# The 56 expert tiles whose first layer is computed early: spread over the dense loop instead of standing at its head

## The chip, the cores and the metric

The kernel runs on one core of a Trainium2 chip. A core has a matrix engine (TensorE, PE in the profile), a vector engine (VectorE, DVE), an engine for activation functions (ScalarE, ACT), a general engine (GpSimd, POOL), a queue engine that only issues transfers (SyncE, SP), and 16 DMA engines that all queues share. The metric is the time of one execution on the device, in microseconds (us); the lower, the better. Each engine works through its own list of instructions in a fixed order, and semaphores hold an instruction back until what it needs is there.

## The reference, cut to what matters

One layer of a hybrid model for two streams of tokens: P (256 prompt tokens) and Q (1024 sample tokens). A token mixer comes first, which this change leaves alone. Then comes PEER, a mixture of 16384 one-neuron experts: each token picks 8 x 16 = 128 experts, and

```python
u = u_tab[idx]
act = jax.nn.gelu(jnp.einsum("td,thkd->thk", xb, u).astype(jnp.float32))
v = v_tab[idx]
return jnp.einsum("thk,thkd->td", (g * act).astype(xb.dtype), v)
```

`u_tab` and `v_tab` hold 16384 rows of 1024 floats each, 64 MiB a table. The result is added to the residual and layer-normed.

## The kernel before, in words

PEER is done in two ways at once.

**Dense.** The first five blocks of 128 tokens of stream Q (`DB = 5`, 640 tokens) go through all experts as matrix products. The 16384 experts are cut into 128 tiles of 128. For tile `n` the first layer (`first_layer`) multiplies a 128 x 1024 tile of `u_tab` (`raw<-in_peer_uT`, split into a high and a low half `uh`, `ul`) with the tokens `hTh`, `hTl`: 2 column halves of 320 tokens, 8 slices of the model dimension, 3 products of halves, so 48 matmuls with 320 columns. A Gelu on ScalarE gives `a`. `weighted(n)` multiplies `a` with the routing weights of the tile, `gt`, which lie in DRAM (`GD`), and splits the product into `wh`, `wl`. `second_layer` multiplies four tiles at a time with the matching tiles of `v_tab` (`vh`, `vl`): 5 token blocks x 2 halves of the output x 4 tiles x 3 products, so 120 matmuls with 512 columns. VectorE adds each result to the accumulators (`acc`, L1108).

The loop over `c` in `dense` makes 32 passes of four tiles. Within pass `c` the four `weighted` calls stand first each time, and the second layer of pass `c - 1` is put between them: token blocks 0 to 2 behind the first, blocks 3 and 4 behind the second. The `v` tiles of pass `c` are loaded and split from the second on; they have four buffers, all of them in use until the second layer of pass `c - 1` ends. The untreated `raw` tiles of `v` have two buffers.

**Early tiles.** For 56 of the 128 tiles (`PRE * 4`, with `PRE = 14`) the first layer is computed ahead of the loop, while the routing and the spreading of the weights of stream Q keep the other engines busy (L1246, L1247); their `a` goes to DRAM (`AD`). In the loop `weighted(n)` only loads it back (L1115). Which tiles these are is what the change touches.

**Gathered.** Stream P's two blocks and Q's blocks 5 to 7 (`experts`) fetch each token's own rows: per block 128 gathers of 128 rows of 4 KB from `in_peer_u` (L1010, issued by GpSimd) with a product and sum on VectorE each (L1023, `row<-row,h`), a Gelu, then 128 gathers from `in_peer_v`, each added with its weight on VectorE (L1032, `y<-row,act,y`). The landing buffers (`row`) are five. After a block's last `y`, `finish` does the layer norm (L984 to L997). Beside the dense loop run the last rows of `in_peer_v` for block 5 and all of blocks 6 and 7, some 580 gathers.

The kernel is written as straight code; a scheduler, which works with an estimate of its own for each duration, lays out every engine's list before the run. So the order in which dense and gathered instructions follow each other on VectorE and GpSimd is fixed when the program is built. `elt` deals the low-half splits (`ul`, `wl`, `vl`, L193) out to VectorE and GpSimd in turn, by a running count of its calls.

After the loop, `dense` multiplies the accumulators with a gate, adds the residual (L1129 on GpSimd, L1130 on VectorE), adds the last pass's products (L1105, L1106), and norms them (L992 to L996).

Of the kernel before, what the change touches and what calls it, by code (L numbers as in the profile page):

```python
# [20 lines left out]
P = 128  # L21
# [3 lines left out]
NK = 128  # L25
# [8 lines left out]


DB = 5
PRE = 14
ADA = 4
MPACE = [(i, ("w_in", int(44 + i * 0.6))) for i in range(16)]
TP, TB = 1, 3  # L40
# [59 lines left out]
def body(ctx, tc, A, O):  # L100
    nc = tc.nc
# [11 lines left out]
    SQ = Stream("Q", 1024, 1, False, "left")  # L113
# [8 lines left out]
    def numbers(pool, n, w):  # L122

        t = pool.tile([P, n, w], BF, name=f"numbers{n}")
        nc.vector.tensor_copy(t[:], iota_k[:, 0:n, None].to_broadcast([P, n, w]))
        return t
# [10 lines left out]
    def bank(s, banks=None):  # L137
        n = count["bank"] = count["bank"] + 1
        banks = banks or s.banks
        return banks[n % len(banks)].tile([P, 512], F32, tag="bank", name=f"bank{n}")  # L140

    def mm(out, terms):
        ops = []
        for l, r in terms:
            if len(l) == 1:
                ops.append((l[0], r[0]))
            else:
                ops += [(l[0], r[0]), (l[0], r[1]), (l[1], r[0])]
        for i, (l, r) in enumerate(ops):
            nc.tensor.matmul(out, l, r, start=(i == 0), stop=(i == len(ops) - 1))  # L150
# [33 lines left out]
    def elt(share):  # L184

        count["lo"] += 1
        n = count["lo"]
        return nc.gpsimd if int(n * share) != int((n - 1) * share) else nc.vector
# [6 lines left out]
    def split(pool, src, shape, tag, bufs=None, eng=None):  # L195
        hi = pool.tile(list(shape), F32R, tag=tag + "h", name=tag + "h", bufs=bufs)
        lo = pool.tile(list(shape), F32R, tag=tag + "l", name=tag + "l", bufs=bufs)
        split_into(hi[:], lo[:], src, eng or nc.gpsimd)
        return hi, lo
# [8 lines left out]
    def sub(op, *idx):  # L208
        return tuple(o[idx] for o in op)

    def dram(name, shape, dt=F32):
        return dp.tile(list(shape), dt, name="d_" + name)
# [4 lines left out]
    def tpool(s, name, bufs=1):  # L217
        return tc.tile_pool(name=name + s.name, bufs=bufs, side=s.side, reuse_waits="tile")
# [681 lines left out]
    def new_T(pool, s, nb):  # L900
        if s.native:
            return (pool.tile([P, KT, nb * P], F32, name="hT"),)
        return (pool.tile([P, KT, nb * P], F32R, name="hTh"), pool.tile([P, KT, nb * P], F32R, name="hTl"))
# [169 lines left out]
    def table(pool, src, tag, bufs, raws, eng):  # L1073

        r = pool.tile([P, D], F32, tag="raw" + tag, name="raw", bufs=raws)
        nc.sync.dma_start(r[:], src)
        return split(pool, r[:], [P, D], tag, bufs=bufs, eng=eng)

    def first_layer(s, T, n, pool, bufs, share):

        U = table(pool, A["peer_uT"][n].rearrange("p k e -> p (k e)"), "u", bufs, 2, elt(share))
        a = pool.tile([P, DB * P], F32, tag="a", name="a", bufs=2)
        for t0 in range(0, DB * P, HALF):
            ts = slice(t0, t0 + HALF)
            ps = bank(s)
            mm(ps[:, :HALF], [(sub(U, ALL, slice(k * P, (k + 1) * P)), sub(T, ALL, k, ts)) for k in range(KT)])
            nc.scalar.activation(a[:, ts], ps[:, :HALF], AF.Gelu_apprx_tanh)
        return a

    def dense(s, T, GD, AD, pool, accs, out):  # L1090
# [19 lines left out]
        def weighted(n):  # L1110
            gt = pool.tile([P, DB * P], F32, tag="gt", name="gt", bufs=3)
            nc.sync.dma_start(gt[:], GD[n])
            if n < PRE * 4:
                a = pool.tile([P, DB * P], F32, tag="a", name="a", bufs=2)
                nc.sync.dma_start(a[:], AD[n])  # L1115
            else:
                a = first_layer(s, T, n, pool, 3, 0.5)
            nc.vector.tensor_tensor(gt[:], a[:], gt[:], op=ALU.mult)  # L1118
            return split(pool, gt[:], [P, DB * P], "w", bufs=6, eng=elt(WSHARE))
# [93 lines left out]
    SQ.banks = everywhere  # L1213
    with tc.tile_pool(name="hcQ", bufs=1, side="right", reuse_waits="tile") as fp:
        hyena(SQ, Matrices(SQ, fp, MPACE), 0.4)
    GD, AD = dram("GD", [NK, P, DB * P]), dram("AD", [PRE * 4, P, DB * P])
    with tpool(SQ, "ya") as ya, tpool(SQ, "w") as wp:
        with tpool(SQ, "yb") as yb:
            halves = {0: ya, 512: yb}
# [4 lines left out]
            Td = new_T(dpool, SQ, DB)  # L1224
# [12 lines left out]
    with (tc.tile_pool(name="rq", bufs=1, side="right", reuse_waits="tile") as rq, tc.tile_pool(name="sp", bufs=1, side="right", reuse_waits="tile") as sp,  # L1237
          tc.tile_pool(name="stage", bufs=1, side="right", reuse_waits="tile") as stage, tc.tile_pool(name="dU", bufs=1, reuse_waits="tile") as up):
        SQ.banks = [pa]
        places, keys8 = numbers(rq, NCAND, TOPK), numbers(sp, NK, 8)  # L1240
        for b in ORDER:
            routes(SQ, [b], rq, places)
            if b < DB:
                spread(SQ, b, sp, stage, keys8, GD)
        SQ.banks = [pb, pc]
        for n in range(PRE * 4):  # L1246
            nc.sync.dma_start(AD[n], first_layer(SQ, Td, n, up, 2, 1)[:])  # L1247
    SQ.banks = everywhere
    ap_ = ctx.enter_context(tc.tile_pool(name="acc", bufs=1, reuse_waits="tile"))
    accs = [ap_.tile([P, D], F32, name=f"acc{b}") for b in range(DB)]  # L1250
# [171 lines left out]
```

## Time and profile before

| what | value |
|---|---|
| median of 3 runs | 5130.33 us (5128.91 to 5131.31) |
| the profiled execution, its own time | 5135.52 us |
| its span, first to last instruction | 5133.7 us |
| PE busy | 4395.7 us, 86% |
| DVE busy | 4081.8 us, 80% |
| POOL busy | 3155.0 us, 61% |
| ACT busy | 2023.5 us, 39% |

The span is what all times in the rows below count in, from its first instruction. The dense loop lies in the last 1530 us: its first matmul starts at 3616.35 us. A share of busy time is a mean over stages with different limits, so the rows below look at stretches of the loop one by one.

### The profile page before, as it was taken

What the parts mean: (1) busy time and instruction counts of PE and PEld (TensorE: products, weight loads), DVE (VectorE), ACT (ScalarE), POOL (GpSimd) and SP (SyncE); (2) the same over time, 40 slices, a digit from 0 to 9 for tenths busy, and PEclk for the clock granted to TensorE, in tenths of its full rate; (3) what the DMA queues carried; (4) which work ended last, traced back from release to release, by engine and by line L of the source; (5) the groups of instructions that cost most, each with busy time, mean ns of one, the idle gap of its engine ahead of it and who ended that gap; (6) DMA issues with size and microseconds to landing.
All of it is one profiled execution on the core that took longest, in us unless ns stands there. A gap on an engine that the chain in (4) does not pass through costs nothing.

```text
span 5133.7 us, 68153 instructions
## 1 busy us (share of the span) xinstructions
PE 4395.7 (86%) x23707; PEld 3804.8 (74%) x23707; DVE 4081.8 (80%) x6816; ACT 2023.5 (39%) x3126; POOL 3155.0 (61%) x2290
## 2 busy tenths in 40 slices
PE   6888788899999779799698887874688999999998
PEld 4676677677777678677587877773566799989997
DVE  7778564999995886566769998895688899888997
ACT  4546333336663112212434766776222222222222
POOL 1456451578886765468665576774556677667764
PEclk8999899999999889899899998995899999999999
DMA  6676646698988953478684478877988999899994
GB/s 212 218 242 196 199 144 234 214 322 293 313 305 320 312 174 99 167 290 327 231 289 153 135 238 267 290 264 245 342 314 322 333 337 340 303 343 337 337 339 155
DMA packets 608774, 1346.80 MB, mean 262 GB/s; under 512 B 63743, under 2 KB 283592, under 8 KB 607917
## 3 DMA queue, kind: packets, MB, share of 16 engines
q0 software_dynamic: 187776, 680.61, 37.7%
q1 hardware_dynamic: 412588, 648.20, 37.6%
q10 hardware_dynamic: 8064, 13.64, 0.7%
q8 instruction: 186, 3.05, 0.2%
q14 instruction: 160, 1.30, 0.1%
HBM read 1177.56 MB, written 164.68 MB: 261 GB/s over the span
## 4 chain that ended last, share of the span: by engine, by line
PE 25%; DVE 15%; DMA 6%; issue 5%; POOL 4%; ACT 3%; SPq 2%; ACTq 0%; POOLq 0%; DVEq 0%
PE bank L150 21%; PE bank L159 3%; DVE row L1023 2%; DVE hot L1058 2%; SPq L1071 2%; POOL row L1010 2%; DVE fi L951 1%; DVE y L1032 1%; DMA row<-in_peer_u,idxQ 1%; ACT G L1069 1%; DMA row<-in_peer_v,idxP 1%; POOL vl L193 1%; ACT oa L1065 1%; ACT ob L1059 1%; DVE gt L1118 1%
## 5 line engine op out<-in xcount | busy, mean ns | idle before, releaser
L1032 DVE SCALAR_TENSOR_TENSOR y<-row,act,y 128x1024 f32<-128x1024 f32 x635 | 814.5, 1283 | 146.4 <-DMA row<-in_peer_v,idxP 111.2
L1023 DVE SCALAR_TENSOR_TENSOR row<-row,h 128x1024 f32<-128x1024 f32 x640 | 762.0, 1210 | 129.2 <-DMA row<-in_peer_u,idxP 60.8
L150 PE MATMUL bank<-hTh,ul 128*128 128x320 f32 x2048 | 641.2, 315 | 16.8 <-POOL ul L193 16.7
L150 PE MATMUL bank<-hTh,uh 128*128 128x320 f32 x2048 | 643.2, 314 | 3.7 <-ACT sc L883 3.6
L150 PE MATMUL bank<-hTl,uh 128*128 128x320 f32 x2048 | 641.9, 314 | 0.0
L150 PE MATMUL bank<-vl,wh 128*128 128x512 f32 x1280 | 513.1, 401 | 50.8 <-POOL vl L193 47.4
L1010 POOL DMA_INDIRECT row<-in_peer_v,idxQ x384 | 409.8, 1067 | 230.9 <-DVE y L1032 176.3
L1010 POOL DMA_INDIRECT row<-in_peer_u,idxQ x384 | 404.9, 1054 | 230.2 <-DVE row L1023 136.3
L150 PE MATMUL bank<-vh,wh 128*128 128x512 f32 x1280 | 473.8, 397 | 76.5 <-ACT vh L192 68.5
L193 POOL TENSOR_TENSOR wl<-wr,wh 128x1024 fp32r<-128x1024 f32 x148 | 362.6, 2451 | 273.7 <-ACT wh L192 252.8
L150 PE MATMUL bank<-vh,wl 128*128 128x512 f32 x1280 | 509.3, 398 | 5.1 <-DVE wl L193 4.9
L150 PEld LDWEIGHTS bank<-hTh,ul 128*128 128x128 f32 x2048 | 390.6, 191 | 20.6 <-POOL ul L193 20.4
L150 PEld LDWEIGHTS bank<-hTh,uh 128*128 128x128 f32 x2048 | 392.0, 191 | 5.7 <-ACT sc L883 3.9
L150 PEld LDWEIGHTS bank<-hTl,uh 128*128 128x128 f32 x2048 | 392.0, 191 | 1.4
L192 ACT ACTIVATE wh<-wr 128x1024 fp32r<-128x1024 f32 x176 | 185.7, 1057 | 463.7 <-PE bank L150 187.6
L1068 PE MATMUL bank<-ob,oa 128*128 128x128 f32 x1280 | 225.6, 327 | 152.2 <-ACT G L1069 74.8
L1010 POOL DMA_INDIRECT row<-in_peer_u,idxP x256 | 272.8, 1065 | 132.3 <-DVE row L1023 73.8
L150 PEld LDWEIGHTS bank<-vh,wh 128*128 128x128 f32 x1280 | 243.8, 191 | 132.7 <-ACT vh L192 72.8
L1010 POOL DMA_INDIRECT row<-in_peer_v,idxP x256 | 277.4, 1083 | 93.7 <-issue 30.6
L150 PEld LDWEIGHTS bank<-vl,wh 128*128 128x128 f32 x1280 | 246.9, 193 | 114.1 <-POOL vl L193 56.5
L1068 PEld LDWEIGHTS bank<-ob,oa 128*128 128x128 f32 x1280 | 196.0, 226 | 179.4 <-ACT G L1069 74.7
L150 PEld LDWEIGHTS bank<-vh,wl 128*128 128x128 f32 x1280 | 246.8, 193 | 59.8 <-DVE wl L193 8.0
(442 smaller groups left out, 12457.6 us busy)
## 6 DMA issues: line engine op xcount, KB each, us to landing
raw<-in_peer_uT SPq DMA_DIRECT2D x128, 512.0 KB
raw<-in_peer_v SPq DMA_DIRECT2D x128, 512.0 KB
wr<-in_w_in SPq DMA_DIRECT2D x112, 512.0 KB
d_GD<-G SPq DMA_DIRECT2D x40, 1024.0 KB
gt<-d_GD SPq DMA_DIRECT2D x128, 320.0 KB
w<-in_w_ada SPq DMA_DIRECT2D x48, 512.0 KB
wr<-in_w_query SPq DMA_DIRECT2D x48, 512.0 KB
d_AD<-a SPq DMA_DIRECT2D x56, 320.0 KB
```

What stands on the lines that cost most here:

```text
L150: nc.tensor.matmul(out, l, r, start=(i == 0), stop=(i == len(ops) - 1))
L159: nc.tensor.matmul(out, a, b, start=(i + j == 0), stop=(i == KT - 1 and j == len(ops) - 1))
L192: nc.scalar.activation(hi, src, AF.Copy)
L193: note(eng, eng.tensor_tensor(lo, src, hi.bitcast(F32), op=ALU.subtract))
L951: nc.vector.tensor_reduce(idf[:, h, :], oh[:].rearrange("p c k -> p k c"), axis=AX.X, op=ALU.add)
L1010: i = nc.gpsimd.indirect_dma_start(out=t[:], out_offset=None, in_=A[tab], in_offset=bass.IndirectOffsetOnAxis(ap=idx[:, k:k + 1], axis=0))
L1023: nc.vector.scalar_tensor_tensor(t[:], t[:], 1.0, h[:], op0=ALU.mult, op1=ALU.mult, accum_out=act[:, k:k + 1])
L1032: nc.vector.scalar_tensor_tensor(y[:], t[:], act[:, k:k + 1], y[:], op0=ALU.mult, op1=ALU.add)
L1058: nc.vector.tensor_tensor(hot[:].rearrange("p k t q -> p k (t q)"), keys8[:], key[:, None, t0:t0 + 4, :].rearrange("p o t q -> p o (t q)") ...
L1059: nc.scalar.activation(ob[:], hot[:, :, :, 1].rearrange("p k t -> p t k"), AF.Copy)
L1068: nc.tensor.matmul(ps[:, i * P:(i + 1) * P], oa[:, i, :], ob[:, i, :], start=True, stop=True)
L1071: nc.sync.dma_start(GD[j:j + 16, :, b * P:(b + 1) * P].rearrange("j i t -> i j t"), G[:, j:j + 16, :])
```

## The change

The list `EARLY` names the tiles with an early first layer. In place of the first 56 tiles it takes the first two of every pass of four, and only the first in each fourth pass: 24 x 2 + 8 x 1 = 56. So passes 0 to 13, which computed no first layer in the loop, and passes 14 to 31, which computed four each, become passes with two, and each fourth with three. The number of early tiles, the work and the data moved stay the same.

```diff
-PRE = 14
+EARLY = [n for n in range(128) if n % 4 < (1 if n // 4 % 4 == 3 else 2)]
...
-            if n < PRE * 4:
+            if n in EARLY:
                 a = pool.tile([P, DB * P], F32, tag="a", name="a", bufs=2)
-                nc.sync.dma_start(a[:], AD[n])
+                nc.sync.dma_start(a[:], AD[EARLY.index(n)])
             else:
                 a = first_layer(s, T, n, pool, 3, 0.5)
...
-    GD, AD = dram("GD", [NK, P, DB * P]), dram("AD", [PRE * 4, P, DB * P])
+    GD, AD = dram("GD", [NK, P, DB * P]), dram("AD", [len(EARLY), P, DB * P])
...
-        for n in range(PRE * 4):
-            nc.sync.dma_start(AD[n], first_layer(SQ, Td, n, up, 2, 1)[:])
+        for i, n in enumerate(EARLY):
+            nc.sync.dma_start(AD[i], first_layer(SQ, Td, n, up, 2, 1)[:])
```

Every engine's list is the same, but for the numbers of the tiles, until the loop's first instructions; behind that the scheduler lays it out anew. Two places show how.

The first is TensorE's list in the middle of the loop, where the second layer of one pass follows that of the pass before it. `bank1203` is the last output of a pass, `bank1204` and `bank1205` are the first ones of the next; `vh_30717`, `vh_30732`, `vh_30738`, `vh_30753` are the high halves of its four `v` tiles. Before:

```order
L150 MATMUL bank1203_30701<-vl_30554,wh_30547 128x512
L150 MATMUL bank1203_30701<-vh_30553,wl_30548 128x512
L150 MATMUL bank1204_30766<-vh_30717,wh_30562 128x512
L150 MATMUL bank1205_30780<-vh_30717,wh_30562 128x512
...
L150 MATMUL bank1204_30766<-vh_30732,wh_30655 128x512
...
L150 MATMUL bank1204_30766<-vh_30738,wh_30726 128x512
...
L150 MATMUL bank1204_30766<-vh_30753,wh_30747 128x512
```

The same place in the changed kernel, where `bank1260` to `bank1263` are the outputs of two first layers, and `vh_32143`, `vh_32215`, `vh_32221`, `vh_32293` the four `v` tiles of the pass that follows:

```order
L150 MATMUL bank1260_32156<-hTh_19688,uh_32151 128x320
...
L150 MATMUL bank1263_32260<-hTh_19688,ul_32230 128x320
L150 MATMUL bank1264_32306<-vh_32143,wh_31988 128x512
L150 MATMUL bank1264_32306<-vl_32144,wh_31988 128x512
L150 MATMUL bank1264_32306<-vh_32143,wl_31989 128x512
L150 MATMUL bank1264_32306<-vh_32215,wh_32081 128x512
L150 MATMUL bank1264_32306<-vl_32216,wh_32081 128x512
L150 MATMUL bank1264_32306<-vh_32215,wl_32082 128x512
L150 MATMUL bank1264_32306<-vh_32221,wh_32209 128x512
...
L150 MATMUL bank1264_32306<-vh_32293,wh_32287 128x512
```

Between the last use of the old `v` tiles and the first use of the new ones there stood nothing; now 96 matmuls of two first layers stand there. From the pass's first second-layer matmul on, the third tile was used after 36 others and the fourth after 54; now after 6 and 33.

The second place is the end of VectorE's list, from the last accumulation of pass 30 (`bank_39691`) to the end of the program. Before:

```order
L1130 SCALAR_TENSOR_TENSOR acc_29490<-spare,acc_29490 128x1024
L1108 TENSOR_TENSOR acc_29493<-acc_29493,bank_39691 128x512
L1130 SCALAR_TENSOR_TENSOR acc_29492<-spare,acc_29492 128x1024
L193 TENSOR_TENSOR vl<-raw,vh 128x1024
...
L995 TENSOR_TENSOR acc_29493<-acc_29493,spare 128x1024
L996 TENSOR_TENSOR acc_29493<-acc_29493,spare 128x1024
L1417 UNCONDITIONAL_BRANCH
```

And in the changed kernel:

```order
L1108 TENSOR_TENSOR acc_29493<-acc_29493,bank_39691 128x512
L1032 SCALAR_TENSOR_TENSOR y<-row,act,y 128x1024
L1130 SCALAR_TENSOR_TENSOR acc_29490<-spare,acc_29490 128x1024
...
L995 TENSOR_TENSOR acc_29493<-acc_29493,spare 128x1024
L1032 SCALAR_TENSOR_TENSOR y<-row,act,y 128x1024
L996 TENSOR_TENSOR acc_29493<-acc_29493,spare 128x1024
L1032 SCALAR_TENSOR_TENSOR y<-row,act,y 128x1024 x17
L984 TENSOR_TENSOR r<-y,spare 128x1024
...
L995 TENSOR_TENSOR r<-r,spare 128x1024
L1417 UNCONDITIONAL_BRANCH
```

Before, no gathered row (`y`) is left behind that accumulation; in the changed kernel 43 are, the last 17 of them behind everything dense, and the gathered block's layer norm (L984 and what follows it) closes the program. In between, a pass with two first layers carries 17 gathered rows on VectorE and one with three carries 21, where passes 2 to 12 carried about 13 and passes 14 to 29 about 25 (fewer where one gathered block ends and the next begins).

## Rows read from the trace of the kernel before

**Rows 1.** The page, part 2: busy tenths in 40 slices of the span.

```profile
PE   6888788899999779799698887874688999999998
```

**Rows 2.** Busy time by stretch: start:end, us, each engine (instructions), PE clock, DMA share, GB/s.

```profile
3612.00:3688.00 76.00, 61.23 (x250) 48.97 (x251) 57.70 (x56) 25.47 (x33) 44.55 (x33) 0.90 0.95 353
3688.00:4064.00 376.00, 318.07 (x1283) 249.58 (x1282) 325.32 (x416) 75.86 (x90) 233.64 (x174) 0.95 0.90 326
...
4164.00:4442.00 278.00, 277.43 (x1559) 252.59 (x1558) 258.87 (x228) 69.71 (x101) 197.12 (x155) 1.00 0.94 335
...
4506.00:5006.00 500.00, 493.03 (x2763) 449.72 (x2762) 447.42 (x525) 124.77 (x181) 353.53 (x282) 0.99 0.94 339
...
5068.00:5134.00 66.00, 43.51 (x217) 37.29 (x215) 55.15 (x76) 17.13 (x24) 24.50 (x9) 0.85 0.27 103
```

**Rows 3.** Waits of PE, 3612 to 4064: us in total, times, longest.

```profile
PE bank L150 <- ACT vh L192: 68.5, 10, 52.2
PE bank L150 <- POOL vl L193: 46.8, 18, 4.9
```

**Rows 4.** Timeline of PE, single matmuls: start, us, what, idle before.

```profile
3616.35 1.22 PE L150 MATMUL bank<-vh,wh 128*128 128x512 f32 x2 [52.16 <-ACT vh L192]
...
4567.41 0.31 PE L150 MATMUL bank<-hTh,uh 128*128 128x320 f32 x1
...
4588.39 0.31 PE L150 MATMUL bank<-hTh,ul 128*128 128x320 f32 x1
...
4588.54 0.40 PE L150 MATMUL bank<-vh,wh 128*128 128x512 f32 x1
...
4604.67 0.39 PE L150 MATMUL bank<-vh,wl 128*128 128x512 f32 x1
...
5067.61 0.39 PE L150 MATMUL bank<-vh,wl 128*128 128x512 f32 x1
```

**Rows 5.** Timeline of PE, from one pass's second layer to the next, near 3760.

```profile
3756.98 0.39 PE L150 MATMUL bank<-vh,wl 128*128 128x512 f32 x1
...
3770.98 0.50 PE L150 MATMUL bank<-vl,wh 128*128 128x512 f32 x1 [2.27 <-POOL vl L193]
...
3777.53 0.50 PE L150 MATMUL bank<-vl,wh 128*128 128x512 f32 x1 [2.18 <-POOL vl L193]
```

**Rows 6.** Groups of DVE, 3612 to the end: count, busy, mean ns, idle before.

```profile
L1032 DVE SCALAR_TENSOR_TENSOR y<-row,act,y 128x1024 f32<-128x1024 f32 x324 | 415.8, 1283 | 23.3 <-DMA row<-in_peer_v,idxQ 19.2
...
L1118 DVE TENSOR_TENSOR gt<-a,gt 128x640 f32<-128x640 f32 x128 | 187.5, 1467 | 45.2 <-DMA a<-d_AD 31.1 <-ACT a L1087 9.7 <-DMA gt<-d_GD 3.2
...
L193 DVE TENSOR_TENSOR wl<-gt,wh 128x640 fp32r<-128x640 f32 x64 | 66.5, 1040 | 13.0 <-ACT wh L192 13.0
...
L1130 DVE SCALAR_TENSOR_TENSOR acc<-spare,acc 128x1024 f32<-128x1024 f32 x5 | 11.8, 2357 | 0.2 <-DMA spare<-d_X1Q 0.2
L1106 DVE TENSOR_TENSOR acc<-acc,t 128x512 f32<-128x512 f32 x10 | 7.5, 766 | 0.0
L995 DVE TENSOR_TENSOR acc<-acc,spare 128x1024 f32<-128x1024 f32 x5 | 7.2, 1441 | 2.6 <-ACT acc L994 2.6
L1105 DVE TENSOR_TENSOR t<-bank,spare 128x512 f32<-128x512 f32 x10 | 6.6, 681 | 1.8 <-PE bank L150 1.8
L992 DVE BATCH_NORM_STATS2 st<-acc 128x6 f32<-128x512 f32 x10 | 6.4, 660 | 0.0
```

**Rows 7.** Waits of DVE, 4164 to 4442.

```profile
DVE y L1032 <- DMA row<-in_peer_v,idxQ: 8.1, 6, 2.3
DVE acc L1108 <- PE bank L150: 4.9, 10, 0.8
```

**Rows 8.** Timeline of DVE: the last gathered row, a block's norm, the last norm.

```profile
4453.22 1.29 DVE L992 BATCH_NORM_STATS2 st<-r 128x6 f32<-128x512 f32 x2
...
5039.52 1.27 DVE L1032 SCALAR_TENSOR_TENSOR y<-row,act,y 128x1024 f32<-128x1024 f32 x1
...
5125.92 0.15 DVE L820 SCALAR_TENSOR_TENSOR mv<-mv 128x1 f32<-128x1 f32 x1
```

## The prediction

> **What bounds the kernel now.** I read the slices first [rows 1]. TensorE is nearly full in the last quarter but dips in the slices before it, so the dense loop has more than one regime; the totals by engine hide that. The table by stretch shows two [rows 2]. From 3688 to 4064, the passes without a first layer, PE is busy 318 of 376 us and no engine is full: DVE 87%, transfers 90%. From 4164 on, the passes with four first layers, PE is busy 277.4 of 278 and 493 of 500 us. So the loop is bound by TensorE in the second regime only. In the first, PE waits for the split `v` tiles [rows 3]: 46.8 us for `vl` on GpSimd and 68.5 for `vh`, of which 52.2 lie before the loop's first matmul. The timeline shows how [rows 5]: the last matmul on the old `v` tiles starts at 3756.98, the third new tile is ready at 3770.98 and the fourth at 3777.53, that is 14.0 and 20.6 us later, and no other matmul stands between.
>
> **Matmul time.** Back to back, 144 first-layer matmuls start from 4567.41 to 4588.39, 0.1467 us apart, and 72 second-layer ones from 4588.54 to 4604.67, 0.2272 us apart [rows 4]. A first layer is 48 x 0.1467 = 7.04 us, a pass's second layer 120 x 0.2272 = 27.26. A pass with two first layers is then 41.34 us, with three 48.4, with four 55.4. Up to the end of pass 30's second layer the loop holds 31 x 27.26 + 70 x 7.04 = 1337.9 us of matmuls, before and after the change alike. It took 3616.35 to 5067.84 [rows 4], 1451.5 us: 113.6 us are lost, nearly all in the start and the first regime.
>
> **What the change removes.** In the first regime the refill of `v` had no cover. Now two first layers, 14.1 us, stand between old and new tiles, then 6 matmuls ahead of the third tile and 33 ahead of the fourth: needed after 15.5 and 21.6 us, ready after 14.0 and 20.6 if the chain is as long as in rows 5. So the gap closes, with 1.0 to 1.5 us to spare. I estimate what stays lost:
> - Start, 10 us: the first first-layer tile has to land and be split, about 5 us behind the old first matmul, and passes 0 and 1 meet the refill with all else still landing. The bounds are 5 and the 14.8 us of idle PE that the first row of rows 2 has.
> - Two changes of gathered block inside the loop, 8 us each, 16 together: the 7 us of idle PE in 4506 to 5006 [rows 2] are about one of them, and the first change now falls in passes as full as these. Bounds 8 and 20.
> - 1% of the remaining 1250 us, 13: the second regime lost 0.2 to 1.4% [rows 2], and the cover is thinner than its 21 us. Bounds 3 and 40 (the rivals).
>
> Pass 30's second layer then ends at 3616.35 + 1337.9 + 39 = 4993.3 in place of 5067.8, 74.6 us earlier.
>
> **What it moves.** The new order leaves 43 gathered rows behind the last accumulation of pass 30, where before the last row was done at 5039.5 [rows 8], 28 us ahead of that point. DVE works its list in order, so all the rest stands in one queue: 43 rows x 1.283 = 55.2; 4 of L1130 x 2.357 = 9.4; ten each of L1105, L1106, L992 at 0.681, 0.766 and 0.660 = 21.1; 5 of L995 x 1.441 = 7.2; two `gt` and two `wl`, 5.0 [rows 6]; the few others and some 20 tiny ones about 7. Together 105 us. I add 2 us by which DVE trails PE and 4 for the last 17 rows: 0.524 MB a row at 353 GB/s, the highest rate in rows 2, is 1.49 us, 0.2 above DVE's 1.283. PE has only 41 us of work left there and is done long before. The last row ends at about 4993.3 + 111 = 5104. Behind it stands the gathered block's norm, which nothing covers any more: two passes of 1.2 us, statistics of 1.29 [rows 8], 1 to 2 us of tiny steps, and the 7.8 us that lay between L820 at 5125.92 and the end of the span, with 1.2 more because GpSimd adds where VectorE did: 14 us. The span ends at 5118.
>
> So the end part grows from 65.9 us (5067.8 to 5133.7) to 125, and of 74.6 us won 59 go back. Change: -15.4 us. The sum is made against the profiled execution, 5133.7 us of span and 5135.5 of its own time; the median of the runs is 5130.3, so I subtract from that: **5115 us**. The new early tiles cost what the old ones did, and loading `a` moves no more bytes; that the lists ahead of the loop are unchanged makes both nothing.
>
> **Transfers.** A pass with two first layers moves 17 rows, four tiles of `v` and two of `u` at 0.524 MB and six of `gt` and `a` at 0.328: 14.0 MB in 41.34 us, 339 GB/s, with all transfers together. The second regime ran at 335 and 339 with PE full, the first at 326 [rows 2]. The Trainium skill (DMA: Bandwidth & Descriptors, "Issuing engines are not separate DMA queues") says that transfers from SP and GpSimd run on the same 16 engines and interleave. By that rule spreading the tiles adds no transfer capacity; the trace agrees, at 0.90 to 0.94 busy in both regimes.
>
> **The rivals.**
> 1. *Transfers hold the mixed loop.* If it gets only the first regime's 326 GB/s, a pass takes 14.0 / 0.326 = 43.0 us in place of 41.34 and one with three first layers 50.0 in place of 48.4. Over the 29 passes from 2 to 30 that is 49 us, 36 beyond the 13 booked: 5151, slower. It decides below 332 GB/s, where the gain is eaten. For it: rows 2 show no more than 339 over any long stretch. Against: PE was full at that. Chance 0.20.
> 2. *The end is paced by transfers or DVE runs full.* If the last 27 rows come at the loop's pace, 41.34 / 17 = 2.43 us, and not at DVE's 1.8 with its other work, 17 us are added: 5132, no change. DVE in the loop points the same way: with `in_peer_v` it was busy 258.9 of 278 us, 51.8 a pass, 33.0 of it for 25.7 rows; 18.8 less one split of 1.2 plus 17 x 1.283 is 39.4 of 41.34, 95%. Its waits for others than PE were 278 - 258.9 - 4.9 = 14.2 us [rows 2, 7], 2.8 a pass; if all stay, 42.2, so 0.9 over in some 14 passes, about what is booked. Chance 0.25.
> 3. *The whole gain comes through.* With the end part as long as before, 74.6 us: 5056. It needs gathers that keep up with the loop, and the order, 43 rows behind it, speaks against that. The Trainium skill (Perfetto Trace Analysis, "Optimization Strategy") says that where the most-contended engine changes over time, interleaving the regimes may help; by it alone this would be the sum. The trace agrees on the two regimes, not on an end that stays as it was. Chance 0.05.
>
> **How the numbers follow.** My forecast has a chance of 0.47, with 5104 to 5126 as its own range (the start and the block changes at their bounds); 0.03 stay unnamed. A measurement of this kernel can tell about 0.2%, 10.3 us: faster is below 5120.1, slower above 5140.6. Of the forecast's 0.47 some 0.09 lie above 5120. Faster: 0.38 + 0.05 + 0.03 = 0.46. Same: 0.09 + 0.25 = 0.34. Slower: 0.20. The range from 5093 to 5150 leaves out rival 3, half of rival 1 and what is unnamed.
>
> **What would show it.** Right: no stretch of the loop with PE below about 95%; pass after pass 41 to 42 us, each fourth 48 to 49; the last accumulation of pass 30 near 4995; then some 110 us in which DVE is full and PE falls idle after 40; the last instruction a norm of gathered rows. Wrong: PE waits for `vl` or `wl` in each pass (the cover was too thin), gathers that let DVE wait in mid-loop (rival 1), or DVE below 85% busy after the last matmul (rival 2). What would upset it most is a delay of 1 us a pass in the chain of rows 5: all 29 passes would pay it.

## The result, and the profile after

The changed kernel takes 5101.45 us (median of 6 runs, 5091.99 to 5110.95) where the kernel before takes 5130.82 in the same runs (5127.26 to 5135.92): a ratio of 0.9942, 95% interval 0.9928 to 0.9956, or 29 us less (22 to 37). The forecast was 5115 us, a change of -15.4. The profiled execution took 5101.32 us with a span of 5099.5; before it was 5133.7.

The slices of the span come first, as in [rows 1]:

```profile
PE   6888788899999779889798887884699999999993
DVE  6778563999995786566769998895588989989998
```

TensorE's slices 30 and 31, the first regime, rose from 8 to 9; its last slice fell from 8 to 3 instead, while VectorE stays at 8 and 9 to the end. Busy time by stretch (start:end, us, each engine with its instructions, clock of PE, DMA share, GB/s), to be held against [rows 2]:

```profile
3612.00:3700.00 88.00, 81.23 (x416) 72.25 (x417) 64.47 (x57) 30.69 (x43) 60.54 (x41) 0.93 0.91 326
3700.00:4036.00 336.00, 328.07 (x1734) 290.79 (x1734) 295.04 (x366) 89.88 (x121) 222.98 (x167) 0.99 0.90 324
4036.00:4500.00 464.00, 462.57 (x2434) 409.90 (x2433) 413.57 (x455) 119.42 (x160) 308.12 (x236) 1.00 0.92 332
4500.00:4560.00 60.00, 57.35 (x314) 51.46 (x313) 52.75 (x77) 16.59 (x23) 43.62 (x34) 1.00 0.94 346
4560.00:4966.00 406.00, 403.80 (x2131) 358.58 (x2130) 373.10 (x439) 100.35 (x136) 289.96 (x220) 1.00 0.93 338
4978.00:5100.00 122.00, 43.85 (x219) 37.84 (x217) 109.60 (x122) 15.62 (x22) 71.83 (x51) 0.70 0.67 233
```

There is one regime now. PE is idle for 14.2 of the 1266 us from 3700 to 4966, and 10.6 of these lie in the two stretches in which a gathered block changes (7.9 and 2.65). The wait in the second one goes back to a row that landed late: VectorE waits for it, and the `gt` product behind it in VectorE's list, the split `wh` and PE's matmul are late with it:

```profile
4511.36 1.22 DVE L1023 SCALAR_TENSOR_TENSOR row<-row,h 128x1024 f32<-128x1024 f32 x1 [4.37 <-DMA row<-in_peer_u,idxQ]
4513.64 0.82 DVE L1118 TENSOR_TENSOR gt<-a,gt 128x640 f32<-128x640 f32 x1
4514.49 0.74 ACT L192 ACTIVATE wh<-gt 128x640 fp32r<-128x640 f32 x1 [2.03 <-DVE gt L1118]
4515.29 0.51 PE L150 MATMUL bank<-vh,wh 128*128 128x512 f32 x1 [2.65 <-ACT wh L192]
```

The last stretch is another picture: PE idle after a third of it, transfers at 0.67, VectorE busy 109.6 of 122 us.

The waits of PE from 3612 to 4990 (what for, us in total, times, longest) answer to [rows 3]:

```profile
PE bank L150 <- ACT uh L192: 54.6, 1, 54.6
PE bank L150 <- ACT wh L192: 11.3, 8, 2.6
...
PE bank L150 <- DVE vl L193: 0.9, 1, 0.9
...
```

The first is the wait for the loop's first tile, ahead of the loop. The 46.8 us for `vl` have become 0.9. PE's timeline (start, us) gives the loop's two ends and PE's last matmul, as [rows 4] did, and the refill of one pass, as [rows 5] did:

```profile
3618.77 0.63 PE L150 MATMUL bank<-hTh,uh 128*128 128x320 f32 x1 [54.64 <-ACT uh L192]
...
4541.03 0.39 PE L150 MATMUL bank<-vh,wl 128*128 128x512 f32 x1
...
4555.34 0.40 PE L150 MATMUL bank<-vh,wh 128*128 128x512 f32 x1
...
4978.20 0.39 PE L150 MATMUL bank<-vh,wl 128*128 128x512 f32 x1
...
5025.34 0.39 PE L150 MATMUL bank<-vh,wl 128*128 128x512 f32 x1
```

Between the last old `v` product at 4541.03 and the first new one at 4555.34 stand 14 us of first layers, and no matmul of that pass shows a wait. Pass 30's second layer ends with the matmul at 4978.20, 89.4 us earlier than at 5067.61 before. From there the span lasts 121.3 us, where it was 66.1.

Not all of these 89 us were waits. The loop from its first matmul to the end of pass 30's second layer, before and after, as a busy time by stretch:

```profile
3616.35:5067.84 1451.49, 1374.45 (x7080) 1203.41 (x7081) 1261.98 (x1443) 353.39 (x484) 968.35 (x744) 0.98 0.91 326
```

```profile
3618.77:4978.43 1359.66, 1345.46 (x7081) 1193.51 (x7082) 1203.84 (x1395) 356.43 (x482) 932.20 (x701) 1.00 0.92 332
```

The same matmuls, 1337.9 us back to back, kept PE busy 36.5 us longer than that before and 7.6 us now; PE's idle time fell from 77.0 to 14.2 us. So 62.8 us of the gain are waits that are gone, 28.9 lie in the matmuls themselves, and 2.4 go back for a first matmul that comes later. The granted clock tells of the second part. Before, matmuls started 0.43 us apart in place of 0.2272 behind some of the waits for `v`, and in such a piece the clock is at the lower of its two levels, 1.2 GHz (0.50 of full speed):

```profile
3737.76 0.50 PE L150 MATMUL bank<-vl,wh 128*128 128x512 f32 x1 [3.16 <-POOL vl L193]
...
3739.78 0.63 PE L150 MATMUL bank<-vh,wl 128*128 128x512 f32 x1
3740.21 0.63 PE L150 MATMUL bank<-vl,wh 128*128 128x512 f32 x1
```

```profile
3739.40:3742.40 3.00, 3.00 (x9) 2.35 (x8) 3.00 (x2) 0.00 (x0) 2.98 (x2) 0.50 1.00 367
```

A mean of 0.95 from 3688 to 4064 [rows 2] is a tenth of that stretch at the lower level; by my estimate from the two spacings this costs up to 18 us there. The rest of the 28.9 us was not taken apart.

VectorE's timeline shows what it is doing, and its waits from 4975 on are few:

```profile
5066.96 7.91 DVE L1032 SCALAR_TENSOR_TENSOR y<-row,act,y 128x1024 f32<-128x1024 f32 x6 [1.15 <-DMA row<-in_peer_v,idxQ]
...
5080.14 5.26 DVE L1032 SCALAR_TENSOR_TENSOR y<-row,act,y 128x1024 f32<-128x1024 f32 x4 [0.19 <-DMA row<-in_peer_v,idxQ]
```

```profile
DVE y L1032 <- DMA row<-in_peer_v,idxQ: 3.3, 6, 1.2
...
```

The last gathered row is added at 5085.4, 60 us behind PE's last matmul; before, it was done 28 us ahead of pass 30's end [rows 8]. Then comes the norm, 14.1 us to the end of the span.

So 89 us were won in the loop and 55 lost behind it (121.3 - 66.1): 34 by the profiled executions, 29 by the medians.

### The profile page after: what moved, and what is told of

It reads as the page before. It is cut to its first block, busy times and chain, and to the rows that moved or that the text cites. A ratio compares the mean times of both kernels' runs of the same rounds, so it can differ in the third digit from the quotient of the medians.

```text
span 5099.5 us, 68083 instructions
## 1 busy us (share of the span) xinstructions
PE 4365.1 (86%) x23707; PEld 3794.9 (74%) x23707; DVE 4083.2 (80%) x6816; ACT 2029.5 (40%) x3124; POOL 3161.3 (62%) x2290
## 4 chain that ended last, share of the span: by engine, by line
PE 21%; DVE 15%; issue 7%; DMA 7%; POOL 4%; ACT 3%; SPq 2%; POOLq 0%; ACTq 0%; DVEq 0%
PE bank L150 17%; PE bank L159 3%; SPq L1071 2%; POOL row L1010 2%; DVE hot L1058 2%; DVE row L1023 2%; DVE y L1032 2%; DMA row<-in_peer_v,idxQ 2%; DVE fi L951 1%; DMA row<-in_peer_u,idxQ 1%; DVE gt L1118 1%; ACT G L1069 1%; DMA row<-in_peer_v,idxP 1%; ACT oa L1065 1%; ACT ob L1059 1%
## 5 line engine op out<-in xcount | busy, mean ns | idle before, releaser
L1010 POOL DMA_INDIRECT row<-in_peer_v,idxQ x384 | 421.2, 1097 | 239.7 <-DVE y L1032 173.2
L150 PE MATMUL bank<-vh,wh 128*128 128x512 f32 x1280 | 499.3, 392 | 15.2 <-ACT wh L192 15.2
L150 PE MATMUL bank<-vl,wh 128*128 128x512 f32 x1280 | 499.2, 391 | 0.9 <-DVE vl L193 0.9
L150 PE MATMUL bank<-vh,wl 128*128 128x512 f32 x1280 | 480.6, 391 | 2.0 <-POOL wl L193 1.8
L192 ACT ACTIVATE wh<-gt 128x640 fp32r<-128x640 f32 x128 | 94.8, 741 | 479.7 <-DVE gt L1118 479.5
```

The costliest lines, as they stand in the source:

```text
L192: nc.scalar.activation(hi, src, AF.Copy)
L1010: i = nc.gpsimd.indirect_dma_start(out=t[:], out_offset=None, in_=A[tab], in_offset=bass.IndirectOffsetOnAxis(ap=idx[:, k:k + 1], axis=0))
```

## The experiments

All times are medians beside the kernel before, run on the same chip. Its median was 5134.2 to 5135.4 us there, and single runs of it lay between 5121 and 5153, so differences between kernels are read from the ratios, and places from the profiles. A profile is one execution: two of the same kernel may differ by some 10 us.

"Pass 30 ends" is the start of its last second-layer matmul, "end part" what is left of the span from there.

| kernel | us | ratio to before (95%) | span | pass 30 ends | end part | rows left behind |
|---|---|---|---|---|---|---|
| before | 5130.82 | | 5133.7 | 5067.61 | 66.1 | 0 |
| changed | 5101.45 | 0.9942 (0.9928 to 0.9956) | 5099.5 | 4978.20 | 121.3 | 43 |
| noblk_b | 5128.78 | 0.9987 (0.9973 to 1.0001) | 5116.6 | 5051.83 | 64.8 | 0 |
| noblk_a | 5042.88 | 0.9816 (0.9794 to 0.9837) | 5044.0 | 4977.96 | 66.0 | 0 |
| early48 | 5112.18 | 0.9956 (0.9939 to 0.9974) | 5111.5 | 5028.63 | 82.9 | 12 |
| early64 | 5113.59 | 0.9966 (0.9953 to 0.9979) | 5110.5 | 4944.90 | 165.6 | 72 |
| first01 | 5111.40 | 0.9950 (0.9933 to 0.9968) | 5104.1 | 4989.03 | 115.1 | 41 |
| nog_b | 4923.47 | 0.9591 (0.9567 to 0.9614) | 4922.0 | 4859.23 | 62.8 | 0 |
| nog_a | 4908.97 | 0.9563 (0.9539 to 0.9586) | 4905.6 | 4843.06 | 62.5 | 0 |
| blk1_b | 5082.97 | 0.9896 (0.9879 to 0.9913) | 5083.5 | 5018.94 | 64.6 | 0 |
| v5u2_b | 5130.23 | 0.9990 (0.9979 to 1.0001) | 5122.8 | 5025.25 | 97.6 | 17 |
| tail1 | 5097.65 | 0.9927 (0.9914 to 0.9939) | 5087.7 | 4973.26 | 114.4 | 43 |
| tail2 | 5109.98 | 0.9944 (0.9932 to 0.9957) | 5109.0 | 4988.71 | 120.3 | 43 |
| wpool | 5114.55 | 0.9954 (0.9934 to 0.9974) | 5114.5 | 4989.24 | 125.3 | 43 |

**Is it the rows left behind that make the end longer?** Both kernels without their last gathered block.

```diff
-        experts(SQ, range(DB, SQ.tt), O["ys"], peer, ready)
+        experts(SQ, range(DB, SQ.tt - 1), O["ys"], peer, ready)
```

> The kernel before, with the third gathered block (tile 7 of Q, the one gathered last) left out: its rows of the output are not computed. My theory: in the changed kernel the loop gains some 89 us and the rows that are left behind the last accumulation of pass 30 give some 60 of them back. Here no rows stood behind it, so leaving the block out should move the loop only by what its second block change cost: pass 30's second layer ends at 5055 to 5068 (5067.8 with the block), and the end part of 66 us shrinks by the gathered norm only, to some 50 to 62. Time 5105 to 5130. Rival (VectorE's gathers slow the second regime): pass 30 ends before 5040.

> The changed kernel, with the same gathered block left out (its rows of the output are not computed). By my theory nothing is left behind the loop now, so the end part is as long as in the kernel before without that block, and the whole gain of the loop is seen: pass 30's second layer ends near 4970, the time is 75 to 95 us below the kernel before without the block, some 5025 to 5045. Rival (the longer end comes from something other than the rows left behind, such as VectorE or GpSimd being behind with the loop's own work): the difference stays near the 29 us of the full kernels, with an end part over 100 us.

With no rows left behind, the change is worth 85.9 us (5128.78 to 5042.88) in place of 29 (72.6 by the spans of the two profiled executions, of which that of `noblk_b` is its fastest), and both kernels have the same end part, 64.8 and 66.0 us. Pass 30 of `noblk_a` ends within 0.3 us of the changed kernel's, from a first matmul 4.8 us later: the rows of that block cost the loop 5 us at most, and the long end is theirs. `noblk_b` ends pass 30 15.8 us earlier than the kernel before; 6.7 of these come from a loop that starts earlier, the other 9 are about the 7 us of idle PE that I had put down to the second change of block in [rows 2].

**Does each row count?** Eight early tiles less, and eight more.

```diff
-EARLY = [n for n in range(128) if n % 4 < (1 if n // 4 % 4 == 3 else 2)]
+EARLY = [n for n in range(128) if n % 4 < (1 if n // 4 % 2 else 2)]
```

```diff
+EARLY = [n for n in range(128) if n % 4 < 2]
```

> The changed kernel with 48 in place of 56 early tiles, spread as evenly: every second pass has three first layers in the loop, the others two. The loop holds 8 x 7.04 = 56.3 us more of matmuls, and only 12 gathered rows are left behind pass 30's last accumulation in place of 43. Theory (the loop is bound by PE, the end by VectorE's list): pass 30's second layer ends 56.3 us later less what the stage ahead of the loop saves by eight tiles less (between 10 and 56 us; I take 30), and the end part shrinks by 31 x 1.283 = 40 us, from 121 to 81. Together 5101.5 + 56 - 30 - 40 = 5088, between 5060 and 5110. Rival (the loop is held by VectorE or transfers rather than by PE): the end of pass 30 hardly moves by the matmuls, since rows and bytes per pass are what counts, and the time falls to about 5040. Second rival (the end part has a length of its own): 5101.5 + 56 - 30 = 5128.

> The changed kernel with 64 in place of 56 early tiles, the first two of each pass, so that each pass has two first layers in the loop. The loop holds 56.3 us less of matmuls, and 72 gathered rows are left behind pass 30's last accumulation in place of 43. Theory: the end of pass 30 comes 56.3 us earlier less what eight more tiles cost ahead of the loop (10 to 56 us; I take 30), and the end part grows by 29 x 1.283 = 37 us to 158: 5101.5 - 56 + 30 + 37 = 5112, between 5085 and 5140. Rival (the end part has a length of its own): 5101.5 - 56 + 30 = 5075, with an end part of 115 to 125.

Pass 30 ends 50.4 us later with 48 and 33.3 us earlier with 64, where its matmuls are 56.3 more or less. The end part moved with the rows: 31 rows less made it 38.4 us shorter (39.8 worked out), 29 more made it 44.3 longer. VectorE waits 10.4 us for rows there in place of 3.3; 29 x 1.283 = 37.2 and these 7.1 are the 44.3:

```profile
DVE y L1032 <- DMA row<-in_peer_v,idxQ: 10.4, 16, 2.0
```

So a loop bound mainly by PE and an end part bound by VectorE's list carry over to other numbers of early tiles, and the two rivals, 5040 or 5128 for `early48` and 5075 for `early64`, fell. The 30 us taken for the stage ahead of the loop were too many. The loop's first matmul, with 48 and then with 64, to be held against 3618.77:

```profile
3600.18 0.64 PE L150 MATMUL bank<-hTh,uh 128*128 128x320 f32 x1 [53.37 <-ACT uh L192]
```

```profile
3631.78 0.64 PE L150 MATMUL bank<-hTh,uh 128*128 128x320 f32 x1 [54.73 <-ACT uh L192]
```

Eight tiles less let the loop start 18.6 us earlier, eight more 13.0 later (kernels with the same work ahead of the loop differ there by up to 17 us, 3608.3 to 3625.4, so both figures are rough). The loop itself took 69.0 us more and 46.3 less where the matmuls are 56.3 more or less, so both lost 10 to 13 us more than the changed kernel, which I cannot explain. `early48` came 24 us above its sum, outside its range. Neither is better than 56.

**Is it the cover of the refill?** The same number of early tiles per pass, but the last ones, so that only one first layer stands between old and new `v` tiles.

```diff
-EARLY = [n for n in range(128) if n % 4 < (1 if n // 4 % 4 == 3 else 2)]
+EARLY = [n for n in range(128) if n % 4 >= (3 if n // 4 % 4 == 3 else 2)]
```

> The changed kernel, with the same 56 tiles per pass spread evenly, but the early ones are the last two of a pass, so that the loop's first layers stand ahead of the second layer's two parts and only one of them, 7.0 us, stands between the last matmul on old v tiles and the first on new ones (in 23 of the 31 passes; two in the other 8). The traffic per pass is the same. My theory (the cover of the refill makes the gain): the third and fourth new tile are needed 8.4 and 14.5 us after the last old matmul and ready after 14.0 and 20.6, so PE waits some 6 us in each of 23 passes, 140 us in all: 5240, between 5190 and 5260, with waits of PE for vl and vh in each pass. Rival (spreading the tiles evens out the transfers, and where in the pass they stand does not matter): 5090 to 5115.

My number was far off: 5111 and not 5240, and PE's waits from 3612 to 4990 are these:

```profile
PE bank L150 <- POOL vl L193: 9.7, 7, 3.0
PE bank L150 <- DVE vl L193: 8.3, 7, 2.2
PE bank L150 <- ACT vh L192: 2.2, 2, 1.1
...
```

I had taken the order of the second layer's matmuls for fixed. It is not: with six output banks the scheduler draws the products of the first two `v` tiles ahead of those of the third. TensorE's list gives, from the last use of the old tile in a buffer to the first use of the new one, by 0.1467 and 0.2272 us a matmul:

| passes | third tile | fourth tile |
|---|---|---|
| before, 1 to 12 | 39 second-layer, 8.9 us | 44 to 54, 10.0 to 12.3 us |
| first01, one first layer | 48 first- and 33 to 39 second-layer, 14.5 to 15.9 us | 15.7 to 18.6 us |
| changed | 96 first- and 9 to 15 second-layer, 16.1 to 17.5 us | 21.6 to 23.6 us |

So 7 us less of first layers took only 1 to 2 us from the third tile's time and 5 to 6 from the fourth's. That PE waits for `vl` and `vh` again, 20 us in all where the changed kernel waits 0.9, is what is left of the test; it cannot tell how much the cover as a whole is worth.

**Cover or traffic?** Both kernels without any gathered block beside the loop (the `noblk` edit with `SQ.tt - 3`).

> The kernel before with all three gathered blocks of the loop left out (their rows of the output are not computed), so the loop moves about half as many bytes and VectorE has little to do. Theory (the first regime loses its time in the refill of the four v tiles, a chain of transfer and split that nothing covers): PE still loses 20 to 50 us between 3688 and 4064, since the third tile's first use stands 39 matmuls or 8.9 us behind the last use of the old one while its chain takes 10 to 14 us; pass 30's second layer ends between 5025 and 5060. Rival (transfers at 90% are what PE waits for in the first regime): with half the bytes PE's loss there falls below 10 us and pass 30 ends near 5000.

> The changed kernel with all three gathered blocks left out (their rows are not computed). Theory: the refill is covered by two first layers with or without the gathers, so PE runs at its matmul time of 1337.9 us from the loop's start to the end of pass 30's second layer, which ends between 4960 and 4975, and what the kernel before without gathers loses more than this is what the cover alone is worth, 40 to 80 us. Rival (transfers): no difference between the two beyond 15 us.

Here the rival is right. Without gathers the loop starts at about 3500, and the passes without a first layer end near 3875 in the kernel before. That stretch, in the kernel before and in the changed one:

```profile
3531.00:3875.00 344.00, 337.38 (x1439) 266.59 (x1438) 175.22 (x214) 79.47 (x97) 104.05 (x49) 1.00 0.51 162
```

```profile
3531.00:3875.00 344.00, 343.68 (x1819) 305.50 (x1818) 141.67 (x147) 89.80 (x124) 88.61 (x41) 1.00 0.38 120
```

With nothing but its own second-layer matmuls as cover, PE is idle for 6.6 us of 344 (12 passes of 28.7 us), not for 58 of 376 as in [rows 2], and its clock stays at 1.00. The change is worth 14.5 us between these two, not 40 to 80. The refill is short unless gathered rows run beside it. Passes with and without rows are best compared in one program, the kernel before with the first gathered block only (the same edit, `SQ.tt - 2`):

> The kernel before with only the first of the three gathered blocks (the rows of the other two are not computed): in the order 70 rows stand in the passes up to pass 5 of the first regime, and none in its last eight, while the v tiles and all matmuls stand as before. It tells what makes the refill chain of 14 to 20 us so long. Theory as corrected by the kernels without gathers (the chain is long because its transfers share the engines with the gathered rows): the first five passes take 33 to 37 us each, the later ones of the same regime 27.3 to 28. Theory as first put (the chain is long by itself): passes with and without rows both take 33 to 36 us.

VectorE's last accumulation of some passes, then PE's stretches with and without rows, and PE's waits in the first:

```profile
3698.46 0.68 DVE L1108 TENSOR_TENSOR acc<-acc,bank 128x512 f32<-128x512 f32 x1
...
3838.23 0.67 DVE L1108 TENSOR_TENSOR acc<-acc,bank 128x512 f32<-128x512 f32 x1
3866.76 0.68 DVE L1108 TENSOR_TENSOR acc<-acc,bank 128x512 f32<-128x512 f32 x1
3894.99 0.68 DVE L1108 TENSOR_TENSOR acc<-acc,bank 128x512 f32<-128x512 f32 x1
```

```profile
3688.00:3840.00 152.00, 130.39 (x532) 102.55 (x531) 133.05 (x135) 31.62 (x38) 85.33 (x63) 0.96 0.85 301
3840.00:4064.00 224.00, 221.85 (x985) 179.27 (x984) 107.11 (x133) 50.85 (x62) 71.27 (x32) 1.00 0.49 158
```

```profile
PE bank L150 <- POOL vl L193: 14.7, 6, 4.6
PE bank L150 <- ACT vh L192: 4.6, 4, 2.0
...
```

Four passes with rows take 139.8 us, 34.9 each; the next two, in the same regime of the same program, 28.5 and 28.2, and PE is idle for 2 of 224 us. Over the 27.26 us of its matmuls a pass without gathers costs 1 to 1.5 us more and one with them 7 to 8, in part at the lower clock (0.96 in the mean).

What makes the refill longer beside the rows can be read from one fourth `v` tile with rows and one without: SyncE issues its transfer, ScalarE makes `vh`, GpSimd makes `vl`.

```profile
3772.30 0.33 SPq L1076 DMA_DIRECT2D raw<-in_peer_v  x1
3778.84 1.06 ACT L192 ACTIVATE vh<-raw 128x1024 fp32r<-128x1024 f32 x1 [2.14 <-DMA raw<-in_peer_v]
3783.93 0.94 POOL L1010 DMA_INDIRECT row<-in_peer_v,idxQ  x1 [0.30 <-DMA row<-in_peer_v,idxQ]
3784.89 2.40 POOL L193 TENSOR_TENSOR vl<-raw,vh 128x1024 fp32r<-128x1024 f32 x1
```

```profile
3869.33 0.33 SPq L1076 DMA_DIRECT2D raw<-in_peer_v  x1
3874.20 1.06 ACT L192 ACTIVATE vh<-raw 128x1024 fp32r<-128x1024 f32 x1 [0.97 <-DMA raw<-in_peer_v]
3876.87 2.98 POOL L193 TENSOR_TENSOR vl<-raw,vh 128x1024 fp32r<-128x1024 f32 x1
```

From issue to `vh` it is 6.5 us with rows and 4.9 without, and from the end of `vh` to the start of `vl` 5.0 and 1.6: with rows, three gathers stand between the third tile's split and the fourth's in GpSimd's list. So the transfer is only part of it; here GpSimd's list makes the larger part, and no run takes the two apart. Leaving rows out removes both, and work of VectorE too. The transfers of the `v` tiles are issued by SyncE and the rows by GpSimd; that the one slows the other agrees with the Trainium skill (DMA: Bandwidth & Descriptors, "Issuing engines are not separate DMA queues"), by which both run on the same 16 engines and interleave.

**Is it then the rate of transfers alone?** The kernel before with a fifth buffer for `v`.

```diff
-            return pool.tile([P, D], F32, tag=("uh", "uh", "uh", "ul", "ul", "ul", "rawu", "rawu", "rawv")[count["spare"]], name="spare", bufs=2 if count["spare"] > 5 else 3)
+            return pool.tile([P, D], F32, tag=("uh", "uh", "vh", "ul", "ul", "vl", "rawu", "rawu", "rawv")[count["spare"]], name="spare", bufs=5 if count["spare"] in (2, 5) else 2)
...
-                a = first_layer(s, T, n, pool, 3, 0.5)
+                a = first_layer(s, T, n, pool, 2, 0.5)
...
-                        V.append(table(pool, A["peer_v"].rearrange("(i j) d -> j i d", j=NK)[4 * c + i], "v", 4, 2, elt(0.5)))
+                        V.append(table(pool, A["peer_v"].rearrange("(i j) d -> j i d", j=NK)[4 * c + i], "v", 5, 2, elt(0.5)))
```

> The kernel before, with a fifth buffer for the two halves of v (vh, vl) in the loop, so that one tile of the refill no longer waits for the last old matmul, and two buffers in place of three for those of u, which makes the room. The first layers stay where they were. My theory (the first regime loses its time in the refill of v): PE's loss between 3688 and 4064 falls from 58 us to under 25, pass 30 ends some 30 to 45 us earlier, near 5030; 17 gathered rows are left behind it in the order, so the end part grows from 66 to some 86 us: 5116, between 5100 and 5135. Rival (the first regime is held by its transfers at 326 GB/s): PE's loss there stays at 45 to 60 us and the time is 5140 to 5160. What two buffers for u cost shows as waits of PE for uh and ul in the second regime, and is to be read apart.

The first regime, and PE's waits from 3612 to 4064:

```profile
3688.00:4064.00 376.00, 338.35 (x1431) 274.16 (x1430) 326.91 (x392) 83.94 (x101) 230.77 (x163) 0.95 0.87 310
```

```profile
PE bank L150 <- ACT vh L192: 63.9, 6, 51.0
PE bank L150 <- POOL vl L193: 28.1, 13, 5.6
...
```

PE loses 37.7 us in place of 58, between the two expectations. Pass 30 ends 42 us earlier, but 17 rows are left behind, the end part is 97.6 (12 beyond the 86 worked out; VectorE waits there 6.5 us for rows and 3.3 for GpSimd), and the timed ratio cannot be told from 1. Not a clean test, since the scheduler gave the first regime's passes about 10 rows each in place of 13. Nor does it settle the question: the 310 GB/s are a mean over the stretch, and a mean does not say whether transfers were full while a `v` tile was on its way.

**Is the end part VectorE's list?** The last pass put as all others, which takes ten instructions off that list (`tail1`); besides, the `wl` splits and the norm's last addition on GpSimd (`tail2`); and the `wl` splits alone (`wpool`).

```diff
-                elif c == 31:
-                    t = pool.tile([P, 512], F32, tag="gt", name="t", bufs=3)
-                    nc.vector.tensor_tensor(t[:], ps[:], vec[0][:, cs], op=ALU.mult)
-                    nc.vector.tensor_tensor(accs[b][:, cs], accs[b][:, cs], t[:], op=ALU.add)
...
                         second_layer(c - 1, *last, b)
+                        if c == 32:
+                            x = spare()
+                            nc.sync.dma_start(x[:], s.X1[b * P:(b + 1) * P, :])
+                            nc.gpsimd.tensor_tensor(accs[b][:], accs[b][:], vec[0][:], op=ALU.mult)
+                            nc.vector.scalar_tensor_tensor(accs[b][:], x[:], ALPHA, accs[b][:], op0=ALU.mult, op1=ALU.add)
```

```diff
-TP, TB = 1, 3
+TP, TB = 1, 5
...
-WSHARE = 0.5
+WSHARE = 1.0
```

> The changed kernel with the last pass put as all others: its ten bank sums are added to the accumulators at once, and the multiplication by the gate and the addition of X1 come after it for each accumulator. This takes ten multiplications of 0.681 us (6.8 us) out of VectorE's list behind pass 30 and lets the gate's five multiplications on GpSimd come later. Theory (the end part is VectorE's list): the end part shrinks from 121 by 5 to 8 us, 5094 to 5098 by the median. Rival (the rows' transfers or GpSimd's issues pace the end): no change, 5101.

> The kernel tail1 and, besides, the splits wl all on GpSimd and the last addition of the norm on GpSimd for all five accumulators (for three so far): four instructions of 1.2 us less in VectorE's list behind pass 30. Theory: 3 to 6 us less than tail1, 5088 to 5094. Rival (GpSimd, busy 80 of 134 us there, becomes the one that is late): as tail1 or slower.

> The changed kernel with all splits of the weighted tiles (wl) on GpSimd in place of every second one, which takes some 60 splits off VectorE in the loop (66 us) and two from its list behind pass 30. Theory (the mixed loop is bound by PE; of VectorE only its list behind pass 30 counts): pass 30's second layer ends within 5 us of 4978, the end part shrinks by 2 to 4 us, the time is 5095 to 5103. Rival (VectorE at 90% holds the mixed loop): pass 30 ends 10 to 24 us earlier, near 5085. If GpSimd becomes late with wl, PE waits for it in each pass, and the time is over 5110.

`tail1` has an end part of 114.4 us, 6.9 less than the changed kernel, where 6.8 were taken off the list, and its median, 5097.65, lies in the range of 5094 to 5098. By its ratio, 0.9927 (0.9914 to 0.9939), it is the fastest of the kernels that compute everything, but the interval overlaps that of the changed kernel, 0.9928 to 0.9956: the gain shows in the profile, not yet in the times. `tail2` takes four more off and has an end part of 120.3, as its rival had it. VectorE's waits there from 4975 on, then in `tail1`:

```profile
DVE y L1032 <- DMA row<-in_peer_v,idxQ: 10.7, 10, 2.9
...
```

```profile
DVE y L1032 <- DMA row<-in_peer_v,idxQ: 4.1, 5, 1.3
...
```

The list is shorter and the rows come later, so what VectorE was relieved of it now waits. GpSimd, which issues the gathers, was given the work; that its lateness is what delays them fits but was not tested by itself. `wpool` gives no sign that VectorE holds the mixed loop, though it loads GpSimd in its place. From 3700 to 4966:

```profile
3700.00:4966.00 1266.00, 1249.44 (x6552) 1106.37 (x6551) 1092.49 (x1271) 325.02 (x438) 944.14 (x706) 0.99 0.91 331
```

VectorE is busy 1092 us there in place of 1134 and GpSimd 944 in place of 865, and pass 30 ends no earlier: 4989, in `tail2` too, 11 us later than in the changed kernel, not the 10 to 24 earlier of the rival. Whether these 11 us are GpSimd's or the scatter between executions stays open. The time, 5114.55, is above the 5095 to 5103 that I had expected.

## Why the prediction was right, and where not

The direction and the two opposite terms were right; the gain is about twice the one forecast, 29 us against 15.4. The time lies in the range of 5093 to 5150, and 3 us below the likeliest case's own, 5104 to 5126.

- **The matmuls and the loop's gain.** From 3616.35 to the end of pass 30's second layer at 4978.43 there are 1362.1 us; less 1337.9 of matmuls, 24.2 are lost. I had booked 39 (10 + 16 + 13). This is the term of the sum that was mis-sized, and I had read the loss as waiting alone: of the 113.6 us before, 36.5 were matmuls slower than back to back, of the 24.2 now 7.6. The start cost 4.7 (a first matmul 2.4 us later, and a first pass of 43.6 us, 3618.77 to its end, where 41.3 are matmuls), the changes of block 10.6, each near its lower bound of 5 and 8; the rest, 8.9 in place of 13, is idle time and stretches in which matmuls ran slower than back to back. The gain is 89 us and not 74.6.
- **Why there was a loss to win back.** "In the first regime the refill of `v` had no cover" is half of it. That "no other matmul stands between" old and new tiles was wrong for the tiles that PE waited for: 39 second-layer matmuls, 8.9 us, stood ahead of the third, and 44 to 54 ahead of the fourth. Without gathered rows the same refill, with this cover alone, costs 1 to 1.5 us a pass (`nog_b`, `blk1_b`); the 14.0 and 20.6 us of [rows 5] were the chain beside 13 rows a pass. What was lost was a refill made long by the gathers, through its transfers and through GpSimd's list, and covered too little. The change covers it with 16 to 17.5 us for the third tile and 21.6 to 23.6 for the fourth, near the 15.5 and 21.6 that I worked out. How much of the gain is cover and how much is that the rows and `v` tiles are spread over longer passes could not be parted: `first01` kept its cover by another order, and `v5u2_b` moved rows.
- **The rows left behind.** 105 us of work for VectorE, 2 of lag and 4 for rows that come late gave 111 from pass 30's end to the last row; 107 were measured (4978.4 to 5085.4), with 3.3 us of waits for rows. The norm took 14.1 (14). The end part is 121.3 (125), and without the rows 66.0 (`noblk_a`). This step stands by size, and by `early48`, `early64` and `tail1`, each with its own number of instructions.
- **Given back.** 55 of 89 us, not 59 of 74.6.
- **Rival 1, transfers hold the mixed loop.** It got 324 to 346 GB/s by stretch and 332 from 3700 to 4966, just the 332 below which it would have decided, and PE hardly waited for a `v` tile. The sign named for it did show: VectorE waited 53.4 us for rows from 3700 to 4966 (32.3 for `in_peer_u`, 21.1 for `in_peer_v`), and one such row cost PE its 2.65 us. It was near, and with 14.2 us of idle PE in all it did not decide. In the kernel before, transfers beside rows were part of what made the refill long.
- **Rival 2, the end paced by transfers or VectorE full.** The last 27 rows waited 3.3 us, not 17. VectorE was busy 90% of the loop, not 95%, and relieving it at GpSimd's cost did not help (`wpool`).
- **Rival 3, the whole gain.** It holds as soon as no row is left behind: 85.9 us between the `noblk` kernels. The Trainium skill's remark that interleaving regimes may help (Perfetto Trace Analysis, "Optimization Strategy") agrees with the loop here; the end that the new order made is outside it.

## What to carry to other kernels

Where two regimes with different bounds follow each other, mixing them pays, but read from the lists what the mixing leaves behind the last shared pass: here every gathered row there gave back 1.24 to 1.53 us, and 55 of 89 us went that way. A wait for a refill has two lengths, that of the chain and that of its cover; take away what runs beside it before the cover is called the cause, and see in the chain which link grew: the transfer, or an instruction that stands behind others in its engine's list. And a wait can cost more than its own length, when the matmuls behind it run at the lower clock. And where a scheduler lays out the lists, an edit that moves one thing moves others (matmuls that took the place of the cover, rows of another pass), so look at the order of each experiment before its time is forecast.

## What the runs showed of the hardware that was not expected

Means over a stretch hid when the transfers were full. In the kernel with one gathered block the DMA share is 0.85 (301 GB/s) in the stretch with rows and 0.49 (158 GB/s) in that without. While the third and fourth `v` tile are on their way, in one pass of each, it is nearly full with rows and not far from it without:

```profile
3768.60:3778.80 10.20, 9.02 (x37) 6.79 (x37) 10.11 (x11) 2.10 (x3) 5.83 (x6) 1.00 0.96 348
3866.90:3874.20 7.30, 7.30 (x32) 6.06 (x33) 4.70 (x6) 2.03 (x3) 1.52 (x1) 1.00 0.84 296
```

The fourth tile took 6.5 us from issue to first use in the one and 4.9 in the other. A pass rose from between 28.2 and 28.5 us to 34.9; that includes GpSimd's later split and matmuls at the lower clock.
